# The attention's query chain in two requests, and the keys' scaling half a piece later

## The chip, the cores and the metric

The kernel runs on one core of a Trainium2 chip. The metric is the device time of one execution in microseconds; for comparison stands the median of several timed executions without a profile. One further execution was taken with the hardware profiler, and all views of the profile come from it. The engines are named as the profile names them: PE is TensorE (matmuls and transposes, PEld its weight loads), ACT is ScalarE, DVE is VectorE, POOL is GpSimd, SP only issues transfers.

## The reference

A decoder trunk of two layers over 256 tokens of width 2048: a retention layer and its MLP, then keys and values from a compressed latent, and an attention layer with its MLP. What the change touches is the attention, with 16 heads, 128 unrotated and 64 rotated columns per head:

```python
    k_nope = rms_norm(kv[..., :MLA_NOPE_DIM], k_nope_norm)
    ...
    c_q = rms_norm(h @ w_dq, q_norm)
    q = (c_q @ w_uq).reshape(b, s, H, MLA_NOPE_DIM + MLA_ROPE_DIM)
    q_nope = rms_norm(q[..., :MLA_NOPE_DIM], q_nope_norm)
    q_pe = apply_rope(rms_norm(q[..., MLA_NOPE_DIM:], q_pe_norm), cos[:, :, None], sin[:, :, None])
    ...
        sc = jnp.einsum('bhqd,bkhd->bhqk', qn, k_nope) + jnp.einsum('bhqr,bkr->bhqk', qp, k_pe)
        sc = sc.astype(jnp.float32) * scale
        sc = jnp.where(kpos[None, :] <= qpos[:, None], sc, -jnp.inf)
        p = jax.nn.softmax(sc, axis=-1).astype(v.dtype)
        return jnp.einsum('bhqk,bkhd->bqhd', p, v)
    ...
    return o @ w_o
```

## The kernel before

**Weights and pieces.** All products run in float32 accuracy from two parts of each operand: a high part (a cast to fp32r on ACT, L188) and a low part, which is what the cast left over (a subtraction on DVE, L189). PE multiplies high by high, high by low and low by high (L248 to L250 in `piece`). A weight matrix comes in pieces. Each piece is one transfer on SP's queue into one of three `raw` buffers and is used in two halves; each half gets a `wh` and a `wl` tile, of which there are five each. A half of the query's up-projection `uq` is 768 columns wide and feeds 12 matmuls; a half of the output projection `wo` has 1024 columns, and 12 matmuls as well. So PE needs the cast and the subtraction of a half before it starts that half.

**What sets the order.** The helper work between the matmuls is asked for by a small clock. `stream` advances it by half a piece after each half (`tick(0.5)`), `later(n, fn)` puts a function n pieces ahead, and it is run, that is, its instructions are recorded, when the clock gets there. From the recorded program the framework makes one queue for each engine and puts neighbours that don't depend on each other in an order of its own; every engine then works through its queue strictly in order. An instruction at the head of a queue that waits holds up everything behind it. Names in the profile are those of the tiles; in the order's rows the first digit behind a name is the head pair b and the second the token tile t.

**Keys.** `keyed` runs once for each of the eight head pairs (two heads each, two token tiles of 128). ACT scales keys and values out of PSUM, DVE squares and sums the keys (L964, L965) and forms mean plus epsilon (`kn_m`, L177), POOL raises it to the power -1/2 (`kn_r`, L178), and DVE scales the keys with it (L970). Two pieces later they are transposed (`kntp`) and split.

**Queries.** `query` runs behind the three pieces of `uq` for each head pair. ACT takes the queries and their squares out of PSUM (L994, L996), DVE sums the squares (L997, L998) and forms mean plus epsilon (`qn_m`), POOL makes the power (`qn_r`), and DVE scales the queries (L1005), rotates the 64 rotated columns (`pe_rope`, L863 to L866) and splits them (`qpp`, L1014, L1015). 3.5 pieces later (2.5 for the last pair) `turn` transposes both parts on PE (`qntp`, `qptp`) and makes `qt` (L1021, then cast and split) and `qpe` (L1026).

**Scores and softmax.** `score` follows 2.5 pieces behind (1.5 and 1 for the last two pairs). PE makes the scores `s` (L1041 to L1046), DVE adds the mask (L1051) and takes the maxima (`mx`, L1056), ACT the exponentials with their sums (L1061), DVE the reciprocals (`inv`, L1062), ACT scales (L1067). Then PE transposes the probabilities (`ptp`, L1074), ACT copies them (`pt`, L1076), `values` multiplies by the values (`ao`, L1085, L1086), and ACT copies the result (`ou`, L1089), which is split for `wo`. `ptp` and `ao` take turns in two PSUM banks, so each must wait until ACT has emptied the bank of the last but one.

Of the kernel before, what the change touches and what calls it, by code (L numbers as in the profile page):

```python
# [16 lines left out]
ALU = mybir.AluOpType  # L17
# [18 lines left out]
P = 128  # L36
NT = 2
# [6 lines left out]
NOPE, ROPE, MV, KVR, QR = 128, 64, 128, 512, 1536  # L44
# [22 lines left out]
def yoco(ctx: ExitStack, tc: tile.TileContext, a):  # L67
    nc = tc.nc
# [3 lines left out]
    def f2k(shape, name, dtype=F32):  # L72
        return pool.tile([P, *shape], dtype, tag="f2k", bufs=14, name=name)

    def small(w, name):
        return pool.tile([P, w], F32, tag="small", bufs=36, name=name)
# [12 lines left out]
    def act_tile(name, dtype=F32R):  # L89

        return pool.tile([P, 2, 2, S], dtype, tag="act", bufs=24, name=name)
# [5 lines left out]
    def later(n, fn):  # L97
        queue.append((clock[0] + n, next(count), fn))
# [60 lines left out]
    def gain(col):  # L159
        return gains[:, col : col + 1]  # L160
# [10 lines left out]
    def rstds(total, sizes, name):  # L171

        w = total.free_size()
        m, r = small(w, f"{name}_m"), small(w, f"{name}_r")
        view = m.rearrange("p (t i h) -> p t i h", t=NT, i=len(sizes))
        for i, n in enumerate(sizes):
            nc.vector.tensor_scalar(view[:, :, i], total[:, :, i], 1.0 / n, EPS, op0=ALU.mult, op1=ALU.add)  # L177
        nc.gpsimd.tensor_tensor(r, m, neg_half[:, :w], op=ALU.pow)  # L178
        return r.rearrange("p (t i h) -> p t i h", t=NT, i=len(sizes))
# [5 lines left out]
    def split(h, l, src, scale=None):  # L185

        if scale is None:
            nc.scalar.copy(h, src)  # L188
            return nc.vector.tensor_tensor(l, src, h.bitcast(F32), op=ALU.subtract)  # L189
        nc.scalar.activation(h, src, AF.Copy, scale=scale)  # L190
        return nc.vector.scalar_tensor_tensor(
            l, src, scale, h.bitcast(F32), op0=ALU.mult, op1=ALU.subtract
        )
# [8 lines left out]
    def transposed(srcs, name):  # L202

        tp = bank("tp", [2, S], name)
        for j in range(2):
            for t in range(NT):
                nc.tensor.transpose(tp[:, j, t * P : (t + 1) * P], srcs(t, j), ident)
        return tp
# [509 lines left out]
    act, r = [], []  # L718
# [3 lines left out]
    def ret_projected(h, qk, gate, v, s):  # L722

        wait = 0 if h else 8

        def keyed(acc):
            ret_rope(acc, qk, f"rk{h}", max(wait - 4, 0))
            later(2 if h else 5.5, ret_scores(h, qk, s))

        gemm_t(a["ret_w_qk"], h * 2, act0, KD, f"rq{h}", lambda acc: ret_rope(acc, qk, f"rq{h}", max(wait - 2, 0)))  # L730
        gemm_t(a["ret_w_qk"], (RH + h) * 2, act0, KD, f"rk{h}", keyed)
# [125 lines left out]
    def pe_rope(dst, u, src, t, i, heads):  # L857


        def tab(j, lo, n):  # L860
            return pe_tabs[t][i][:, j, lo : lo + n].unsqueeze(1).to_broadcast([P, heads, n])

        nc.vector.tensor_tensor(dst, src, tab(0, 0, 64), op=ALU.mult)  # L863
        nc.vector.tensor_tensor(u[:, :, 0:32], src[:, :, 32:64], tab(1, 0, 32), op=ALU.mult)
        nc.vector.tensor_tensor(u[:, :, 32:64], src[:, :, 0:32], tab(1, 32, 32), op=ALU.mult)
        nc.vector.tensor_tensor(dst, dst, u, op=ALU.add)  # L866
# [85 lines left out]
    def keyed(acc, b):  # L952
        if b % 2 == 0:
            vs.append(act_tile(f"v{b}", F32))
        vt = vs[-1][:, b % 2].rearrange("p t (h c) -> p t h c", h=2)
        v_s.append(vt)
        kr = []
        s2 = small(2 * NT, f"skn{b}").rearrange("p (t i h) -> p t i h", t=NT, i=1)
        for t in range(NT):
            src = acc[t].rearrange("p (h c) -> p h c", h=2)  # L960
            k = f2k([2, 2, NOPE], f"kn{b}{t}")
            nc.scalar.activation(k[:, 0], src[:, :, 0:NOPE], AF.Copy, scale=rc[t])
            nc.scalar.activation(vt[:, t], src[:, :, NOPE:], AF.Copy, scale=rc[t])
            nc.vector.tensor_tensor(k[:, 1], k[:, 0], k[:, 0], op=ALU.mult)  # L964
            nc.vector.reduce_sum(s2[:, t, 0], k[:, 1], axis=AX.X)  # L965
            kr.append(k)
        rn = rstds(s2, [NOPE], f"kn{b}")
        for t in range(NT):
            k = kr[t]
            nc.vector.tensor_tensor(  # L970
                k[:, 1], k[:, 0], rn[:, t, 0].unsqueeze(2).to_broadcast([P, 2, NOPE]), op=ALU.mult
            )

        def turn():
            tp = transposed(lambda t, j: kr[t][:, 1, j], f"kntp{b}")
            kt = act_tile(f"kt{b}")
            split(kt[:, 0], kt[:, 1], tp, gain(G_KN))
            k_t.append(kt)

        later(2, turn)  # L980

    for b in range(8):
        gemm(a["mla_w_kv_up"], b, ckv, 4, 512, f"ku{b}", lambda acc, b=b: keyed(acc, b))
# [3 lines left out]
    o_act = []  # L987

    def query(acc, b):
        qr, qu = [], []  # L990
        sq = small(4 * NT, f"sq{b}").rearrange("p (t i h) -> p t i h", t=NT, i=2)
        for t in range(NT):
            q = f2k([2, 192], f"qs{b}{t}")
            nc.scalar.activation(q.rearrange("p h c -> p (h c)"), acc[t], AF.Copy, scale=rq[t])  # L994
            u = f2k([2, 192], f"qu{b}{t}")
            nc.scalar.activation(u.rearrange("p h c -> p (h c)"), acc[t], AF.Square, scale=rq[t])  # L996
            nc.vector.reduce_sum(sq[:, t, 0], u[:, :, 0:NOPE], axis=AX.X)  # L997
            nc.vector.reduce_sum(sq[:, t, 1], u[:, :, NOPE:], axis=AX.X)  # L998
            qu.append((q, u))
        r = rstds(sq, [NOPE, ROPE], f"qn{b}")  # L1000
        for t in range(NT):
            q, u = qu[t]
            for i, cols in enumerate((slice(0, NOPE), slice(NOPE, NOPE + ROPE))):
                n = cols.stop - cols.start
                nc.vector.tensor_tensor(  # L1005
                    q[:, :, cols], q[:, :, cols], r[:, t, i].unsqueeze(2).to_broadcast([P, 2, n]), op=ALU.mult
                )
            flat = u.rearrange("p h c -> p (h c)")
            pe = flat[:, 0 : 2 * ROPE]
            tmp = flat[:, 2 * ROPE : 4 * ROPE].rearrange("p (h c) -> p h c", h=2)  # L1010
            pe_rope(pe.rearrange("p (h c) -> p h c", h=2), tmp, q[:, :, NOPE:], t, 1, 2)
            parts = f2k([2, 2, ROPE], f"qpp{b}{t}", F32R)
            pe = pe.rearrange("p (h c) -> p h c", h=2)
            nc.vector.tensor_copy(parts[:, :, 0], pe)  # L1014
            nc.vector.tensor_tensor(parts[:, :, 1], pe, parts[:, :, 0].bitcast(F32), op=ALU.subtract)  # L1015
            qr.append((q, parts.bitcast(F32)))

        def turn():
            tp = transposed(lambda t, j: qr[t][0][:, j, 0:NOPE], f"qntp{b}")
            raw = f2k([2, S], f"qt{b}")  # L1020
            nc.scalar.activation(raw, tp, AF.Copy, scale=gqn)  # L1021
            qt = [f2k([2, S], f"qt{b}{i}", F32R) for i in range(2)]
            split(qt[0], qt[1], raw)
            tp = transposed(lambda t, j: qr[t][1][:, j].rearrange("p i c -> p (i c)"), f"qptp{b}")
            qpe = f2k([2, S], f"qpe{b}", F32R)
            nc.scalar.copy(qpe, tp)  # L1026
            later(2.5 if b < 6 else (1.5 if b < 7 else 1), lambda: score(b, qt, qpe))

        later(2.5 if b == 7 else 3.5, turn)

    def score(b, qt, qpe):

# [60 lines left out]
    for b in range(8):  # L1093
        gemm(a["mla_w_uq"], b * 3, cq, 12, Q_NB, f"uq{b}", lambda acc, b=b: query(acc, b))

    ss = square_sums(NB, "ss3")
    act, r = [], []
# [107 lines left out]
```

## Time and profile before

| | us |
|---|---|
| timed executions (three) | 2480.28, 2480.34, 2482.13; median 2480.34 |
| profiled execution, device time | 2490.9 |
| its span, first to last instruction | 2489.1 |
| keys' up-projection on PE begins | 1505.6 |
| `uq` begins | 1552.6 |
| first `wo` product, behind the scores of pair 5 | 1685.3 |
| `wo` in pairs (`wop`) begins | 1752.3 |
| DVE idle until POOL's `qn_r`, eight times | 13.5 |
| mean granted clock of PE over the span | 0.996 |

The profiled execution is 10.6 us longer than the median of the timed ones; what is read off the profile is compared with its own time. A row of the timeline gives start and length in us, engine, source line, operation, the tile written and those read, and, in brackets, how long the engine sat idle before it and which instruction ended that. A row of stretches gives the bounds, the length, then for each engine its busy time and its number of instructions, the granted clock of PE (1.00 is full), the share of the DMA engines and GB/s.

### The profile page before, as it was taken

The numbers are of one execution on the slowest core, as the hardware profiler recorded it, in microseconds if no ns is written. First come the engines' busy times: TensorE is split into PE (matmuls) and PEld (weight loads), VectorE is DVE, ScalarE is ACT, GpSimd is POOL, SyncE is SP. The second block draws the span as 40 slices with busy tenths as digits, with TensorE's granted clock in tenths as the row PEclk, the third lists the DMA queues.
The fourth block names the chain that finished last, engine by engine and source line by source line (L and its number), as shares of the span: only waits on it lengthen the run. The fifth ranks groups of instructions, "written<-read, shape, count | busy, mean of one in ns | idle before, by whom it ended". The sixth has DMA issues, their size and how long they took to land.

```text
span 2489.1 us, 31657 instructions
## 1 busy us (share of the span) xinstructions
PE 2458.4 (99%) x11614; PEld 2064.2 (83%) x11614; DVE 2199.3 (88%) x2894; ACT 1647.9 (66%) x2301; POOL 232.0 (9%) x287
## 2 busy tenths in 40 slices
PE   9999999999999999999999999999999999999999
PEld 7888887888888888888888888997888788888887
DVE  7899989989899989989999998776999899899896
ACT  6566656556676767666667777666677567676663
POOL 6200001000000010010110001100000100100100
PEclk9999999999999999999999999999999999999999
DMA  8555568555565685785785565444555866866864
GB/s 311 201 196 190 200 190 252 190 194 207 197 236 187 201 251 207 226 238 197 245 261 204 190 207 177 156 148 156 192 204 200 237 214 199 252 201 225 256 212 167
DMA packets 93403, 521.04 MB, mean 209 GB/s; under 512 B 11072, under 2 KB 12224, under 8 KB 40000
## 3 DMA queue, kind: packets, MB, share of 16 engines
q1 hardware_dynamic: 71856, 472.83, 54.2%
q0 software_dynamic: 21248, 46.15, 8.8%
q8 instruction: 91, 1.49, 0.2%
q14 instruction: 64, 0.52, 0.1%
q10 hardware_dynamic: 144, 0.05, 0.0%
HBM read 479.14 MB, written 39.85 MB: 209 GB/s over the span
## 4 chain that ended last, share of the span: by engine, by line
PE 81%; DVE 7%; DMA 5%; issue 3%; POOL 2%; ACT 2%; DVEq 0%; SPq 0%; ACTq 0%; POOLq 0%
PE u_c L365 7%; PE u_c L366 6%; PE u_c L364 6%; PE d_c L365 5%; PE d_c L366 5%; PE d_c L364 5%; PE rp_c L365 3%; PE rp_c L366 3%; PE rp_c L364 3%; PE rk_acc L276 2%; PE rq_acc L276 2%; PE u_p L366 2%; PE u_p L365 2%; DMA d_raw<-in_mlp_w 2%; PE u_p L364 2%
## 5 line engine op out<-in xcount | busy, mean ns | idle before, releaser
L189 DVE TENSOR_TENSOR d_wl<-d_raw,d_wh 128x1024 fp32r<-128x1024 f32 (+1 forms) x256 | 279.1, 1115 | 27.8 <-ACT d_wh L188 27.8
L188 ACT CAST d_wh<-d_raw 128x1024 fp32r<-128x1024 f32 (+1 forms) x256 | 241.8, 975 | 83.6 <-PE d_c L366 49.5
L189 DVE TENSOR_TENSOR u_wl<-u_raw,u_wh 128x1024 fp32r<-128x1024 f32 (+1 forms) x256 | 277.3, 1111 | 16.8 <-ACT u_wh L188 16.8
L188 ACT CAST u_wh<-u_raw 128x1024 fp32r<-128x1024 f32 (+1 forms) x256 | 240.6, 972 | 70.3 <-PE u_c L366 51.0
L365 PE MATMUL u_c<-u_wl,n 128*128 128x512 f32 x712 | 278.6, 391 | 4.0 <-DVE u_wl L189 4.0
L364 PE MATMUL u_c<-u_wh,n 128*128 128x512 f32 x712 | 278.9, 392 | 0.0
L366 PE MATMUL u_c<-u_wh,n 128*128 128x512 f32 x712 | 278.0, 391 | 0.0
L365 PE MATMUL d_c<-d_wl,hid 128*128 128x512 f32 x660 | 257.8, 391 | 4.1 <-DVE d_wl L189 4.0
L364 PE MATMUL d_c<-d_wh,hid 128*128 128x512 f32 x660 | 259.1, 393 | 0.0
L366 PE MATMUL d_c<-d_wh,hid 128*128 128x512 f32 x660 | 257.7, 390 | 0.0
L188 ACT CAST u_wh<-u_u 128x1024 fp32r<-128x1024 f32 x104 | 107.7, 1054 | 112.0 <-DVE u_u L328 53.3
L188 ACT CAST d_wh<-d_u 128x1024 fp32r<-128x1024 f32 x100 | 104.0, 1055 | 100.4 <-DVE d_u L328 55.8
L365 PEld LDWEIGHTS u_c<-u_wl,n 128*128 128x128 f32 x712 | 134.1, 188 | 33.9 <-DVE u_wl L189 6.7
L366 PEld LDWEIGHTS u_c<-u_wh,n 128*128 128x128 f32 x712 | 134.0, 188 | 27.6
L364 PEld LDWEIGHTS u_c<-u_wh,n 128*128 128x128 f32 x712 | 134.2, 188 | 27.4
L365 PEld LDWEIGHTS d_c<-d_wl,hid 128*128 128x128 f32 x660 | 124.4, 189 | 31.2 <-DVE d_wl L189 6.0
L188 ACT CAST rp_wh<-rp_raw 128x1024 fp32r<-128x1024 f32 x112 | 103.9, 945 | 66.3 <-PE rp_c L366 43.1
L366 PEld LDWEIGHTS d_c<-d_wh,hid 128*128 128x128 f32 x660 | 124.2, 188 | 25.7
L364 PEld LDWEIGHTS d_c<-d_wh,hid 128*128 128x128 f32 x660 | 124.4, 188 | 25.4
L189 DVE TENSOR_TENSOR u_wl<-u_u,u_wh 128x1024 fp32r<-128x1024 f32 x104 | 124.0, 1220 | 9.5 <-ACT u_wh L188 9.4
L189 DVE TENSOR_TENSOR rp_wl<-rp_raw,rp_wh 128x1024 fp32r<-128x1024 f32 x112 | 118.4, 1085 | 4.1 <-ACT rp_wh L188 3.9
L189 DVE TENSOR_TENSOR d_wl<-d_u,d_wh 128x1024 fp32r<-128x1024 f32 x100 | 118.9, 1219 | 2.5 <-ACT d_wh L188 2.4
(566 smaller groups left out, 6579.0 us busy)
## 6 DMA issues: line engine op xcount, KB each, us to landing
u_raw<-in_mlp_w SPq DMA_DIRECT2D x128, 1024.0 KB, 5.5
d_raw<-in_mlp_w SPq DMA_DIRECT2D x120, 1024.0 KB, 4.9
rp_raw<-in_ret_w_gv SPq DMA_DIRECT2D x56, 1024.0 KB, 4.9
ro_raw<-in_ret_w_out SPq DMA_DIRECT2D x32, 1024.0 KB, 5.0
uq_raw<-in_mla_w_uq SPq DMA_DIRECT2D x24, 768.0 KB, 4.2
rq_raw<-in_ret_w_qk SPq DMA_DIRECT2D x16, 1024.0 KB, 5.4
rk_raw<-in_ret_w_qk SPq DMA_DIRECT2D x16, 1024.0 KB, 4.9
xh<-d_c POOLq DMA_DIRECT2D x48, 256.0 KB, 6.2
```

The costliest lines, as they stand in the source:

```text
L188: nc.scalar.copy(h, src)
L189: return nc.vector.tensor_tensor(l, src, h.bitcast(F32), op=ALU.subtract)
L276: nc.tensor.matmul(acc[f], wh[:, cols], a.rearrange("p i s -> p (i s)"), start=k == 0, stop=k == nk - 1)
L364: nc.tensor.matmul(dst, ah, bh, start=n == 0, stop=False)
L365: nc.tensor.matmul(dst, ah, bl, start=False, stop=False)
L366: nc.tensor.matmul(dst, al, bh, start=False, stop=n == total[key] - 1)
```

## The change

`query` ends with the request for the power. Scaling, rotation and split become a function `rotated`, asked for 1.5 pieces later (1 for the last pair). `turn` is asked for by `rotated`, 2 pieces behind it (1.5 for the last pair), so it keeps its place at 3.5 (2.5) pieces. In `keyed` the scaling of the keys is asked for half a piece later; its `turn` stays at 2 pieces. No instruction is added or taken away on any engine, and the queues of SP and POOL keep their order.

```diff
--- before.py
+++ after.py
@@ -965,11 +965,15 @@
             nc.vector.reduce_sum(s2[:, t, 0], k[:, 1], axis=AX.X)
             kr.append(k)
         rn = rstds(s2, [NOPE], f"kn{b}")
-        for t in range(NT):
-            k = kr[t]
-            nc.vector.tensor_tensor(
-                k[:, 1], k[:, 0], rn[:, t, 0].unsqueeze(2).to_broadcast([P, 2, NOPE]), op=ALU.mult
-            )
+
+        def normed():
+            for t in range(NT):
+                k = kr[t]
+                nc.vector.tensor_tensor(
+                    k[:, 1], k[:, 0], rn[:, t, 0].unsqueeze(2).to_broadcast([P, 2, NOPE]), op=ALU.mult
+                )
+
+        later(0.5, normed)
 
         def turn():
             tp = transposed(lambda t, j: kr[t][:, 1, j], f"kntp{b}")
@@ -987,7 +991,7 @@
     o_act = []
 
     def query(acc, b):
-        qr, qu = [], []
+        qu = []
         sq = small(4 * NT, f"sq{b}").rearrange("p (t i h) -> p t i h", t=NT, i=2)
         for t in range(NT):
             q = f2k([2, 192], f"qs{b}{t}")
@@ -998,6 +1002,10 @@
             nc.vector.reduce_sum(sq[:, t, 1], u[:, :, NOPE:], axis=AX.X)
             qu.append((q, u))
         r = rstds(sq, [NOPE, ROPE], f"qn{b}")
+        later(1 if b == 7 else 1.5, lambda: rotated(b, qu, r))
+
+    def rotated(b, qu, r):
+        qr = []
         for t in range(NT):
             q, u = qu[t]
             for i, cols in enumerate((slice(0, NOPE), slice(NOPE, NOPE + ROPE))):
@@ -1026,7 +1034,7 @@
             nc.scalar.copy(qpe, tp)
             later(2.5 if b < 6 else (1.5 if b < 7 else 1), lambda: score(b, qt, qpe))
 
-        later(2.5 if b == 7 else 3.5, turn)
+        later(1.5 if b == 7 else 2, turn)
 
     def score(b, qt, qpe):
 
```

What that does to the queues is seen at three places; in the rows of the change the lines below the edit stand 8 higher.

DVE at the end of the query stage, around pair 7's mean (`qn7_m`) and pair 5's mask (`p50`, `p51`). Before, these rows stand behind the whole of pair 7's rotation, whose first row (`qs70`) needs the power of `qn7_m`:

```order
L866 TENSOR_TENSOR qu71_15629<-qu71_15629 128x128
L189 TENSOR_TENSOR wo01_wl1_15890<-wo01_raw_15853,wo01_wh1_15889 128x1024
L1014 COPY qpp71_15653<-qu71_15629 128x2x64
L1051 TENSOR_TENSOR p50_15677<-s5_15656,cst_62 128x256
L1015 TENSOR_TENSOR qpp71_15653<-qu71_15629,qpp71_15653 128x2x64
L1051 TENSOR_TENSOR p51_15678<-s5_15656,cst_62 128x512
L1056 TENSOR_REDUCE mx5_15681<-p50_15677 128x2
L1056 TENSOR_REDUCE mx5_15681<-p51_15678 128x2
L189 TENSOR_TENSOR qt61_15729<-qt6_15726,qt60_15728 128x512
```

Now:

```order
L177 TENSOR_SCALAR qn7_m_15633<-sq7_15620 128x2x2
L1059 TENSOR_TENSOR p50_15659<-s5_15638,cst_62 128x256
L177 TENSOR_SCALAR qn7_m_15633<-sq7_15620 128x2x2
L1059 TENSOR_TENSOR p51_15660<-s5_15638,cst_62 128x512
L1064 TENSOR_REDUCE mx5_15663<-p50_15659 128x2
L1064 TENSOR_REDUCE mx5_15663<-p51_15660 128x2
L1013 TENSOR_TENSOR qs70_15621<-qs70_15621,qn7_r_15634 128x2x128
L1013 TENSOR_TENSOR qs70_15621<-qs70_15621,qn7_r_15634 128x2x64
L1013 TENSOR_TENSOR qs71_15627<-qs71_15627,qn7_r_15634 128x2x128
```

Mask and maxima of pair 5 have moved ahead of pair 7's scaled queries, right behind the mean; `qt61` and the low part `wo01_wl1` follow behind the rotation.

DVE in pair 2's rotation, at the low part of the second half of pair 3's last piece of `uq` (`uq32_wl1`: the digits are the pair and its piece, the 1 the second half). Before:

```order
L1051 TENSOR_TENSOR p01_14586<-s0_14564,cst_62 128x512
L1056 TENSOR_REDUCE mx0_14589<-p00_14585 128x2
L1056 TENSOR_REDUCE mx0_14589<-p01_14586 128x2
L189 TENSOR_TENSOR qt11_14631<-qt1_14628,qt10_14630 128x512
L189 TENSOR_TENSOR uq32_wl1_14710<-uq32_raw_14691,uq32_wh1_14709 128x768
L1062 RECIPROCAL inv0_14591<-den0_14590 128x4
L189 TENSOR_TENSOR uq40_wl0_14817<-uq40_raw_14814,uq40_wh0_14816 128x768
```

Now:

```order
L1070 RECIPROCAL inv0_14573<-den0_14572 128x4
L189 TENSOR_TENSOR qt11_14613<-qt1_14610,qt10_14612 128x512
L1022 COPY qpp20_14663<-qu20_14531 128x2x64
L1022 COPY qpp21_14672<-qu21_14537 128x2x64
L1023 TENSOR_TENSOR qpp20_14663<-qu20_14531,qpp20_14663 128x2x64
L1023 TENSOR_TENSOR qpp21_14672<-qu21_14537,qpp21_14672 128x2x64
L189 TENSOR_TENSOR uq32_wl1_14710<-uq32_raw_14691,uq32_wh1_14709 128x768
L189 TENSOR_TENSOR uq40_wl0_14799<-uq40_raw_14796,uq40_wh0_14798 128x768
```

The low part stood ahead of the softmax's reciprocal; now it stands behind the reciprocal, behind the split `qt11` and behind the four rows of `qpp`.

ACT at the same place, with the semaphores that a row waits for. Before:

```order
L188 COPY uq32_wh0_14693<-uq32_raw_14691 128x768 [waits DMAHW7_49,DVE_49]
L188 COPY uq32_wh1_14709<-uq32_raw_14691 128x768 [waits DVE_49,PE_49]
L1021 ACTIVATE qt1_14628<-qntp1_14623,gqn_86 128x512 [waits DVE_49,PE_49]
L188 COPY qt10_14630<-qt1_14628 128x512 [waits Activation_49]
L1061 ACT_TABLE_LOAD
L1061 ACTIVATE p00_14585,den0_14590<-p00_14585,mx0_14589 128x128 [waits DVE_49]
L1061 ACTIVATE p00_14585,den0_14590<-p00_14585,mx0_14589 128x128
```

Now:

```order
L188 COPY uq32_wh0_14693<-uq32_raw_14691 128x768 [waits DMAHW7_49,DVE_49]
L1069 ACT_TABLE_LOAD [waits DVE_49]
L1069 ACTIVATE p00_14567,den0_14572<-p00_14567,mx0_14571 128x128 [waits Activation_49]
L1069 ACTIVATE p00_14567,den0_14572<-p00_14567,mx0_14571 128x128
L1069 ACTIVATE p01_14568,den0_14572<-p01_14568,mx0_14571 128x256 [waits DVE_49]
L1069 ACTIVATE p01_14568,den0_14572<-p01_14568,mx0_14571 128x256
L1029 ACTIVATE qt1_14610<-qntp1_14605,gqn_86 128x512 [waits PE_49]
L1075 ACTIVATE p00_14567<-p00_14567,inv0_14573 128x128 [waits DVE_49]
L1075 ACTIVATE p00_14567<-p00_14567,inv0_14573 128x128 [waits Activation_49]
L1075 ACTIVATE p01_14568<-p01_14568,inv0_14573 128x256 [waits Activation_49] x2
L188 COPY qt10_14612<-qt1_14610 128x512 [waits Activation_49]
L188 COPY uq32_wh1_14709<-uq32_raw_14691 128x768
```

The table for the exponentials and the exponentials themselves moved ahead of the cast `uq32_wh1` and of `qt1`, and the table load now carries a wait for DVE. Near the end of the stage ACT's row for `wo02_wh0`, which stood behind the copies `pt50` and `pt51`, stands ahead of them.

## The prediction

> **What bounds the kernel now.** I began with the page's busy times:
>
> ```profile
> span 2489.1 us, 31657 instructions
> PE 2458.4 (99%) x11614; PEld 2064.2 (83%) x11614; DVE 2199.3 (88%) x2894; ACT 1647.9 (66%) x2301; POOL 232.0 (9%) x287
> ```
>
> PE (TensorE) sets the time: only where PE waits, or runs at a lower clock, can another order of the same work win or lose. So the second view is what PE waited for from 1500 to 1760 us, the stretch that the change touches (total, times, longest):
>
> ```profile
> PE ptp L1074 <- ACT p L1067: 3.6, 2, 3.4
> PE ptp L1074 <- ACT ou L1089: 2.2, 3, 0.9
> PE ao L1085 <- ACT pt L1076: 1.0, 1, 1.0
> PE ptp L1074 <- ACT qpe L1026: 0.3, 2, 0.2
> ```
>
> All of it is at the transposes of the softmax (ptp) and the product behind them (ao); nothing stands there for the keys. The third view, busy time by stretch (after the bounds: length, PE, PEld, DVE, ACT, POOL, then the granted clock), prices it:
>
> ```profile
> 1642.80:1696.90 54.10, 51.44 (x312) 47.51 (x311) 39.83 (x104) 36.72 (x75) 9.22 (x11) 1.00 0.50 170
> 1695.96:1699.38 3.42, 1.24 (x6) 0.70 (x4) 3.02 (x8) 1.50 (x7) 0.00 (x0) 1.00 0.96 380
> 1696.90:1709.62 12.72, 8.14 (x32) 7.00 (x31) 6.53 (x9) 8.50 (x20) 0.00 (x0) 0.60 0.56 208
> 1700.56:1709.62 9.06, 7.84 (x30) 7.00 (x31) 4.28 (x4) 5.82 (x10) 0.00 (x0) 0.50 0.39 128
> 1945.14:1948.55 3.41, 1.44 (x7) 0.88 (x6) 3.38 (x4) 0.88 (x2) 0.00 (x0) 1.00 0.05 14
> 1948.55:1951.96 3.41, 3.41 (x9) 2.65 (x9) 3.41 (x5) 1.06 (x2) 0.85 (x1) 0.50 0.65 171
> ```
>
> Idle PE: 54.10 - 51.44 = 2.66 us, then 12.72 - 8.14 = 4.58 us. After the second gap the granted clock is 0.50, for 9.06 us of which 7.84 are work.
>
> The fourth view is the timeline of that gap, on PE, DVE, ACT and POOL:
>
> ```profile
> 1696.59 0.39 PE L249 MATMUL wo_acc<-wo_wl,ot 128*128 128x512 f32 x1
> 1696.82 0.39 PE L250 MATMUL wo_acc<-wo_wh,ot 128*128 128x512 f32 x1
> 1700.56 0.48 PE L1074 MATMUL ptp<-cst,p 128*128 128x128 f32 x1 [3.36 <-ACT p L1067]
> 1701.25 1.33 PE L1074 MATMUL ptp<-cst,p 128*128 128x128 f32 x5 [0.21 <-ACT p L1067]
> 1703.91 1.22 PE L1085 MATMUL ao<-pt,v 128*128 128x256 f32 x2 [1.01 <-ACT pt L1076]
> ...
> 1690.01 0.29 DVE L177 TENSOR_SCALAR qn_m<-sq 128x4 f32<-128x4 f32 x2
> 1692.08 0.96 DVE L1005 TENSOR_TENSOR qs<-qs,qn_r 128x256 f32<-128x256 f32 x3 [1.78 <-POOL qn_r L178]
> 1696.24 0.42 DVE L1051 TENSOR_TENSOR p<-s,cst 128x256 f32<-128x256 f32 x1
> 1697.38 1.00 DVE L1056 TENSOR_REDUCE mx<-p 128x2 f32<-128x256 f32 x2
> 1699.77 0.18 DVE L1062 RECIPROCAL inv<-den 128x4 f32<-128x4 f32 x1 [0.80 <-ACT p L1061]
> ...
> 1697.88 0.40 ACT L1061 ACTIVATE p<-p,mx 128x128 f32<-128x128 f32 x1 [6.25 <-DVE mx L1056]
> 1699.64 0.56 ACT L1026 CAST qpe<-qptp 128x512 fp32r<-128x512 f32 x1
> 1700.11 1.49 ACT L1067 ACTIVATE p<-p,inv 128x128 f32<-128x128 f32 x4
> ...
> 1690.38 1.66 POOL L178 TENSOR_TENSOR qn_r<-qn_m,neg_half 128x8 f32<-128x8 f32 x1 [18.02 <-DVE qn_m L177]
> ```
>
> DVE stood 1.78 us behind POOL's power for the last head pair (pair 7), then did that pair's rotation, and only then the mask (p<-s) of pair 5, though PE had computed pair 5's scores before the wo products that end here. ACT sat 6.25 us for the maxima, PE 3.36 us for ACT.
>
> **The change part by part.**
>
> *The last gap.* The new order has p50 right behind the mean of pair 7, at 1690.1 instead of 1696.24. From p50 to the first exponential took 1697.88 - 1696.24 = 1.64 us, so that starts at 1691.8, on an idle ACT; four take 1699.64 - 1697.88 = 1.76, to 1693.5. The power ends at 1692.04, hidden behind masks and maxima (1696.24 to 1698.38). Scaling the probabilities (1.49) ends by 1695.5, with 0.5 allowed for qt6 that now stands before it, while PE's last wo product (0.23 apart) is issued until 1697.05. The row of 3.6 us goes.
>
> *The wait that comes instead.* ao4 takes the PSUM bank of ptp50, so pt50's copy must be done. ACT's order now has the cast of wo02 ahead of that copy, and the cast needs the buffer that PE gives back at the end of the same wo product:
>
> ```profile
> 1704.12 1.05 ACT L188 CAST wo_wh<-wo_raw 128x1024 fp32r<-128x1024 f32 x1
> 1703.38 0.84 ACT L1076 COPY pt<-ptp 128x384 f32<-128x384 f32 x2
> ```
>
> A cast of 1.05 and one copy of about 0.5, against what PE has to do from ptp50 to ao4: 1703.91 - 1700.56 - 0.21 - 1.01 = 2.13 us at half clock, 1.07 at full. PE waits about 0.5, where it waited 1.01; I take 0.5 (0 to 1.0).
>
> *The half clock* goes with the gap: 7.84 us of work at 0.50 take 3.92 at full clock, so 3.92. The stretches to 1699.38 and 1948.55 had PE busy 1.24 and 1.44 of 3.4 us, and the clock was 0.50 behind both; through the short waits of 1642.80 to 1696.90 it was 1.00. Waits of 0.5 to 1 leave 2.4 busy or more, so none follows.
>
> *The three short waits.* The 2.66 us are the rows of ou and qpe (2.2 and 0.3) and rounding. ptp's second bank waited for ou, which ACT copied behind the softmax. Exponentials and scaling now start 1696.24 - 1690.1 = 6 us earlier in each pair, so this idle goes too (0 to 2.66). Idle time also hides a part of each wait: from 1697.05 to 1700.56 are 3.51 us and 3.36 are shown. For eight waits at 0.15, 1.2 us (0 to 1.6).
>
> *What is late next: the low part of a piece's second half.* uq32_wl1, uq62_wl1 and so on now stand on DVE behind softmax, rotation, the reciprocal and qt's split, which wait for ACT. The rows (busy and mean ns by group; then for pair 5 of the queries its mean and PE's first use of the low part):
>
> ```profile
> L1021 ACT ACTIVATE qt<-qntp,gqn 128x512 f32<-128x512 f32 x7 | 4.9, 699 | 0.0
> L188 ACT CAST qt<-qt 128x512 fp32r<-128x512 f32 x7 | 4.3, 612 | 0.1
> L189 DVE TENSOR_TENSOR qt<-qt,qt 128x512 fp32r<-128x512 f32 x7 | 4.8, 688 | 1.3 <-ACT qt L188 1.3
> L1015 DVE TENSOR_TENSOR qpp<-qu,qpp 128x128 fp32r<-128x128 f32 x16 | 4.5, 284 | 0.0
> ...
> 1650.31 0.29 DVE L177 TENSOR_SCALAR qn_m<-sq 128x4 f32<-128x4 f32 x2
> 1659.95 0.33 PE L249 MATMUL uq_acc<-uq_wl,cq 128*128 128x384 f32 x1
> ```
>
> From 1650.4: exponentials from 1652.1 to 1653.9, then qt 0.70, scaling 1.49, cast 0.61, split 0.69, four qpp at most 1.1, the low part 0.95: 5.5 us laid end to end, 1659.4; neighbours on an engine overlap by about 0.1 each (the four scalings start 0.3 to 0.4 apart), so nearer 1658.7. Before 1659.95 either way: no wait in pairs 3 to 7. In pair 2 the chain is longer, by ACT's table load, which now waits for the first maximum, and by a slower power:
>
> ```profile
> 1594.55 2.31 POOL L178 TENSOR_TENSOR qn_r<-qn_m,neg_half 128x8 f32<-128x8 f32 x1 [11.05 <-DVE qn_m L177]
> 1596.90 0.96 DVE L1005 TENSOR_TENSOR qs<-qs,qn_r 128x256 f32<-128x256 f32 x3 [1.53 <-POOL qn_r L178]
> 1598.62 1.28 ACT L1061 ACT_TABLE_LOAD   x1
> 1602.70 0.95 DVE L189 TENSOR_TENSOR uq_wl<-uq_raw,uq_wh 128x768 fp32r<-128x768 f32 x1
> 1605.73 0.33 PE L249 MATMUL uq_acc<-uq_wl,cq 128*128 128x384 f32 x1
> ```
>
> p00 at 1597.4 (two of the three qs), its maximum 1598.8, table 1600.1, exponentials 1601.9, and the same 5.5, less the overlaps 4.7: 1606.6 to 1607.4, where PE wants it at 1605.73. A wait of 0.8 to 1.6; I take 0.8, as in pair 5.
>
> The power is 2.31 there, with a split of uq beside it, and 1.66 beside an idle DVE. The Trainium skill ("SBUF — State Buffer", section "Who interferes with whom") says that a DVE instruction with two SBUF inputs shuts out GpSimd's reads; by that rule the masks, which read PSUM and one SBUF operand, leave the power at 1.66. Stretched by 0.65 all the same, the power would end at 1692.7 and the low parts come 0.65 later at most, about level with PE's use.
>
> *The keys.* Sixteen products move half a piece behind kn_r. DVE waited 4.9 us there in all, PE never:
>
> ```profile
>   DVE kn L970: 4.9, 8
> ```
>
> PE's work covers it, and the transposes of the keys keep 1.5 pieces behind it: 0; without that cover it would be up to 4.9. The orders of SP and POOL, their DMAs among them, stay as they were.
>
> *Sum against the profiled execution (2490.9 us, 2489.1 of them the span):* 2.66 + 4.58 + 3.92 + 1.2 = 12.4 gained, 0.5 + 0.8 = 1.3 paid, net 11.1: 2479.8. The timed runs have a median of 2480.34, 10.6 below the profiled one; I take the same gain there: **2469.2 us**.
>
> **The rivals.**
>
> *The timed runs had no half clock (0.12).* The clock rows are of one execution, and no timed run shows its clock. Against it, 1.24 busy of 3.42 is lower than in the other stretch that lost its clock, and the gap is in every run. Then the gain is 11.1 - 3.9 = 7.2: 2473.1. The Trainium skill ("TensorE: Matmul & The Clock Gate", section "HAM oscillation — how this bites in real kernels") has the clock fall after idle gaps over about 3.4 us; by that the gap of 3.36 is a borderline case. The trace differs: 1.97 us idle of 3.41 were enough at 1948.55.
>
> *Late low parts: slower (0.06).* If ACT comes to the exponentials 4 us later than I put it, in pairs 2 to 7, the low parts are done 2.7 us after PE's use in each: 2480.3 - 11.1 + 6 x 2.7 = 2485.4. It decides from the point where the low part ends behind PE's use (1659.95 for pair 5). For it: qt and the casts on ACT wait for PE's transposes and buffers. Against it: ACT idled 6.25 us exactly there.
>
> *The gap moves (0.12).* ao4, or a low part, waits some 3 us and the clock halves again: 3 + 3.9 come back, and with a second such wait up to 10; 2475 to 2480. For it: ao4's bank hangs on two releases in a row. Against it: the cast and the copy need 1.55 us, no more. That the program does not do what the edit says is excluded by its order, where p50 stands ahead of the scaled queries.
>
> **How the numbers follow.** The forecast has 0.70. Its own terms reach from 12.4 + 0.4 = 12.8 (nothing paid, all hidden parts) to 11.2 - 1.0 - 1.6 = 8.6 (none hidden, both new waits at their bounds): 2467.5 to 2471.8. The range adds the first rival, the nearer part of the third, and 1.5 us below for the spread of the timed runs: **2466.0 to 2476.0**. Within 0.2% (5.0 us; less can't be told from no change in this kernel) begins at 2475.4: two thirds of the third rival, 0.08. Slower 0.06. Faster: 0.70 + 0.12 + 0.04 = 0.86.
>
> **What would show it.** In the changed profile: DVE's qs without waits for POOL from pair 3 on; ACT's first exponential of pair 5 without a wait near 6 us; PE with no idle at ptp, about 0.5 at ao4 and 0.8 at the low part of uq3; a clock of 1.00 from 1680 to 1720. Wrong if PE waits at the low parts of several pairs, if ao4 waits over 1.5 us, or if the clock still halves in this stage.

## The result, and the profile after

| | before | changed |
|---|---|---|
| median of 13 executions each (one of the changed kernel's is the profiled one), us | 2480.34 (2475.36 to 2487.55) | 2473.35 (2461.8 to 2478.78) |
| ratio, 95% interval | | 0.9963 (0.9948 to 0.9978) |
| profiled execution, device time / span, us | 2490.9 / 2489.1 | 2474.0 / 2472.2 |
| first `uq` product to first `wop` product, us | 199.6 | 188.7 |
| mean granted clock over the span | 0.996 | 1.000 |

The change is faster by 0.37%, 9.2 us with an interval of 5.5 to 12.9 (2480.34 times one minus each bound of the ratio; the ratio is that of the means, and the two medians lie only 7.0 us apart). The forecast was 2469.2 us, within 2466.0 to 2476.0; the median measured, 2473.35, lies in that range. The forecast gain was 11.1 us. Over the whole program the spread of single executions is about as large as the gain, so the sharper measure below is the **stretch** from the first `uq` product to the first `wop` product, read off PE's timeline in each profile. Its ends in the changed kernel:

```profile
1554.71 0.42 PE L248 MATMUL uq_acc<-uq_wh,cq 128*128 128x384 f32 x1
...
1743.45 0.48 PE L364 MATMUL wop_c<-wop_wh,ot 128*128 128x512 f32 x1
```

They are 188.7 us apart, 10.9 less than before. The two profiled spans differ by 16.9; the other 6 us lie outside the stretch, in parts that the change leaves alone. Behind it the profile of before has PE waits of 7.0 us and two clock halvings, the changed one waits of 2.7 us and none. These are not the change's.

PE's waits between 1500 and 1760 us (total, times, longest) are now these, in place of four rows with 7.1 us:

```profile
PE uq_acc L249 <- DVE uq_wl L189: 0.9, 1, 0.9
PE ao L1093 <- ACT pt L1084: 0.5, 1, 0.5
```

All waits at ptp are gone. The two that are left are those that the prediction named, 0.8 and 0.5 there. The busy times in the corresponding stretches (length, PE, PEld, DVE, ACT, POOL, clock, DMA share, GB/s), moved by the 2.1 us by which `uq` begins later:

```profile
1644.90:1699.00 54.10, 53.64 (x334) 51.06 (x333) 43.39 (x109) 41.48 (x88) 9.22 (x11) 1.00 0.60 206
1699.00:1720.00 21.00, 21.00 (x122) 18.30 (x121) 11.25 (x20) 14.45 (x37) 0.00 (x0) 1.00 0.42 152
```

PE idles 54.10 - 53.64 = 0.46 us where it idled 2.66, and after that not at all, and the clock stays at 1.00. The place of the last gap, on the timeline of the changed kernel:

```profile
1683.58 0.59 ACT L998 ACTIVATE qs<-uq_acc,cq_r 128x384 f32<-128x384 f32 x1
1684.58 0.40 PE L248 MATMUL wo_acc<-wo_wh,ot 128*128 128x512 f32 x1
1686.22 0.41 DVE L1059 TENSOR_TENSOR p<-s,cst 128x256 f32<-128x256 f32 x1
1687.74 0.40 ACT L1069 ACTIVATE p<-p,mx 128x128 f32<-128x128 f32 x1 [2.15 <-DVE mx L1064]
1688.49 0.96 DVE L1013 TENSOR_TENSOR qs<-qs,qn_r 128x256 f32<-128x256 f32 x3 [0.27 <-POOL qn_r L178]
1696.37 0.82 PE L1082 MATMUL ptp<-cst,p 128*128 128x128 f32 x6
```

The mask of pair 5 starts before the scaled queries of pair 7, ACT waits 2.15 us for the maxima instead of 6.25, and the transposes (ptp) follow without a wait. But note the first two rows. ACT takes pair 7's queries out of PSUM at 1683.58, 1.0 us before the first `wo` product. Before the change it did so 2.2 us after that product:

```profile
1685.25 0.40 PE L248 MATMUL wo_acc<-wo_wh,ot 128*128 128x512 f32 x1
1687.46 0.57 ACT L994 ACTIVATE qs<-uq_acc,cq_r 128x384 f32<-128x384 f32 x1
```

So the whole chain of the last pair began 3.2 us earlier on PE's own scale. The prediction had left it where it was. Whether the last gap was the last pair's own, as predicted, or was handed on from the pairs before it is what most of the experiments are about.

### The profile page after: what moved, and what is told of

Read it like the earlier page. It is cut to its first block, busy times and chain, and to the rows that moved or that the text cites. A ratio compares the mean times of both kernels' runs of the same rounds, so it can differ in the third digit from the quotient of the medians.

```text
span 2472.2 us, 31666 instructions
## 1 busy us (share of the span) xinstructions
PE 2450.6 (99%) x11614; PEld 2059.0 (83%) x11614; DVE 2196.2 (89%) x2894; ACT 1648.7 (67%) x2301; POOL 233.6 (9%) x287
## 3 DMA queue, kind: packets, MB, share of 16 engines
q8 instruction: 91, 1.49, 0.2%
## 4 chain that ended last, share of the span: by engine, by line
PE 86%; DVE 6%; DMA 4%; POOL 2%; issue 1%; ACT 1%; SPq 0%; DVEq 0%; ACTq 0%
PE u_c L365 6%; PE u_c L366 6%; PE u_c L364 6%; PE d_c L365 6%; PE d_c L366 6%; PE d_c L364 6%; PE rp_c L364 3%; PE rp_c L366 3%; PE rp_c L365 3%; PE rk_acc L276 2%; PE rq_acc L276 2%; DMA u_raw<-in_mlp_w 2%; PE d_p L364 2%; PE d_p L365 2%; PE d_p L366 2%; PE u_p L364 2%
```

## The experiments

Each kernel was profiled once. "Stretch" is always from the first `uq` to the first `wop` product. The price of the half clock is half of the PE work that ran at 0.50 inside the stretch, and "at full clock" is the stretch without it. Ratios are to the kernel before, run on the same chip. The kernels split for some pairs only have the keys' scaling where the change has it.

| run | ratio (95%) | stretch | half clock costs | at full clock |
|---|---|---|---|---|
| before | | 199.6 | 3.9 | 195.7 |
| before again | 0.9998 (0.9985 to 1.0012) | 199.3 | 3.8 | 195.5 |
| keys only | 1.0002 (0.9991 to 1.0012) | 198.3 | 2.7 | 195.6 |
| the change | 0.9963 (0.9948 to 0.9978) | 188.7 | 0 | 188.7 |
| query only | 0.9961 (0.9948 to 0.9975) | 188.8 | 0 | 188.8 |
| pair 7 only | 0.9979 (0.9970 to 0.9988) | 195.2 | 1.7 | 193.5 |
| pairs 0 to 6 | 0.9970 (0.9956 to 0.9985) | 190.8 | 0 | 190.8 |
| no power | 0.9955 (0.9938 to 0.9972) | 189.4 | 0 | 189.4 |
| later still | 0.9963 (0.9948 to 0.9978) | 188.7 | 0 | 188.7 |
| many gaps | 1.0375 (1.0352 to 1.0398) | 188.7 | 0 | 188.7 |
| pair 6 only | 1.0003 (0.9987 to 1.0019) | 195.1 | 1.5 | 193.6 |
| pairs 0 to 5 | 0.9989 (0.9977 to 1.0001) | 195.5 | 2.8 | 192.7 |
| from pair 3 on | 0.9958 (0.9941 to 0.9975) | 187.5 | 0 | 187.5 |
| both new waits off | 0.9955 (0.9940 to 0.9969) | 186.8 | 0 | 186.8 |

**Before, again.** No edit.

> The kernel before, unchanged, profiled a second time. It asks how much of what the first profile showed comes back. If the gaps belong to the order of the queues: the stretch from the first uq product to the first wop product is again 199.7 us (within 0.5), PE waits 3.4 us at ptp for pair 5's probabilities, and ratio 1.000. If the half clock behind the gap is an accident of where the gap falls: the clock stays 1.00 there this time, and the stretch is about 195.8 (199.7 less the 3.9 us of half clock).

The gaps came back to a tenth of a microsecond: the four rows of PE's waits between 1500 and 1760 us are those that the prediction shows, figure for figure. So did the half clock behind them. In the stretches of this second profile PE is busy 1.38 us of 3.4, then the clock is 0.50 for 10.2 us with 7.65 us of work:

```profile
1702.10:1705.50 3.40, 1.38 (x7) 0.80 (x5) 3.15 (x8) 1.34 (x7) 0.00 (x0) 1.00 0.91 307
1705.50:1715.70 10.20, 7.65 (x30) 6.81 (x31) 4.46 (x5) 7.15 (x15) 0.00 (x0) 0.50 0.51 186
```

So the stretch is a steady measure (199.6 and 199.3), while the whole span is not (2489.1 and 2484.7).

**The keys alone, and the queries alone.** The first leaves `query` as it was; the second puts the keys' scaling back (the edit shown is the second's):

```diff
-        later(0.5, normed)
+        normed()
```

> Only the keys' scaling is moved; the query chain stands as before. Theory: PE never waited for the keys, so 0: stretch uq to wop 199.7, ratio 1.000, DVE's 4.9 us behind kn_r shorter but worth nothing. Rival: part of the gain comes from here, up to 4.9 us, ratio down to 0.998.

> Only the query chain is split; the keys' scaling stands at its old place. Theory: the whole gain, stretch 188.7 us as in the change, the same two waits (0.9 at the low part of uq3, 0.5 at ao4), ratio as the change has it, 0.996. Rival (the keys matter): stretch 0.5 us or more longer than 188.7.

The keys' part is worth nothing: the stretch at full clock is that of before, the ratio 1.0002. Even DVE's wait, expected to shrink, stayed (total, times, longest):

```profile
DVE kn L972 <- POOL kn_r L178: 4.9, 8, 1.1
```

The stretch itself came out 1.3 us shorter than before's, though PE's waits were the same. Its profile shows why: this time the clock was at 0.50 for 6.8 us and not 10.2.

```profile
1703.10:1709.90 6.80, 5.46 (x20) 4.62 (x20) 3.58 (x3) 5.10 (x10) 0.00 (x0) 0.50 0.34 106
1709.95:1713.00 3.05, 3.05 (x22) 2.84 (x22) 1.83 (x4) 0.79 (x2) 0.00 (x0) 1.00 0.56 236
```

The queries' part alone gives the whole gain, with the same two waits of 0.9 and 0.5.

**The last pair alone, and all but the last.** In the first the split is made for pair 7 only, in the second for 0 to 6 only:

```diff
-        later(1 if b == 7 else 1.5, lambda: rotated(b, qu, r))
+        if b == 7:      # second kernel: b < 7
+            later(1 if b == 7 else 1.5, lambda: rotated(b, qu, r))
+        else:
+            rotated(b, qu, r)
```

with `turn` kept at its old distance from `query` in both, and the keys' scaling half a piece later as in the change.

> The query chain is split for pair 7 alone; pairs 0 to 6 and the keys... the keys' scaling stays half a piece later. My prediction's account: the last gap comes from pair 7's own rotation standing ahead of pair 5's mask, so the 3.4 us at ptp and the half clock go (8.5 us), the three short waits of 2.7 us stay: stretch about 199.7 - 8 = 191.7. Rival (the lateness is handed on from pair to pair: ACT takes pair 7's queries out of PSUM late because pair 4's softmax came late): mask and maxima come earlier but ACT is late all the same, PE still waits 2 us or more at ptp or ao4, stretch 193 or more; if the clock still halves, 196.

> The reverse: the query chain is split for pairs 0 to 6, and pair 7 stands as before, its rotation ahead of pair 5's mask. My prediction's account: the short waits go (2.7 us and hidden parts) and the last gap stays with its half clock: stretch about 199.7 - 3.5 + 0.9 = 197, and PE still waits 3.4 us at ptp50. Rival (the lateness is handed on): with pair 4's softmax on time ACT takes pair 7's queries out earlier, the gap at ptp50 shrinks to 1 us or less, some 1.6 us remain at ao4, no half clock: stretch 190 to 191.

Pair 7 alone: the wait at ptp50 is gone, but 2.3 us stand at ao4, and the short waits are all there (total, times, longest):

```profile
PE ao L1097 <- ACT pt L1088: 2.3, 1, 2.3
PE ptp L1086 <- ACT ou L1101: 2.2, 3, 0.9
PE ptp L1086 <- ACT qpe L1038: 0.7, 3, 0.3
```

On its timeline the mask stands early, as the order has it, yet ACT takes the queries 2.2 us after the first `wo` product, as before:

```profile
1684.90 0.40 PE L248 MATMUL wo_acc<-wo_wh,ot 128*128 128x512 f32 x1
1687.10 0.58 ACT L998 ACTIVATE qs<-uq_acc,cq_r 128x384 f32<-128x384 f32 x1
1688.72 0.41 DVE L1063 TENSOR_TENSOR p<-s,cst 128x256 f32<-128x256 f32 x1
...
1697.36 2.94 ACT L188 CAST wo_wh<-wo_raw 128x1024 fp32r<-128x1024 f32 x3
1700.20 0.85 ACT L1088 COPY pt<-ptp 128x384 f32<-128x384 f32 x2
1700.73 0.70 PE L1097 MATMUL ao<-pt,v 128*128 128x256 f32 x2 [2.27 <-ACT pt L1088]
```

ACT, still late, had three casts of `wo` to make up, 2.94 us of them ahead of the copy of pt50, and ao4 waited for that. In the changed kernel the same row of casts had caught up with PE: the last of them waits 0.98 us for a `wo` product. The clock was 0.50 for one stretch of 3.4 us behind the wait at ao4. The forecast of 191.7 was missed by 3.5 us, though the softmax itself came as the prediction had it: the first exponential 6.0 us after the first `wo` product, where the prediction's 1691.8 is 6.5.

All but the last: pair 7's rotation still stands ahead of the mask, and the gap is gone all the same:

```profile
PE ao L1097 <- ACT pt L1088: 1.4, 1, 1.4
PE uq_acc L249 <- DVE uq_wl L189: 0.9, 1, 0.9
PE ptp L1086 <- ACT p L1079: 0.5, 2, 0.4
```

On the timeline ACT takes pair 7's queries 1.0 us before the first `wo` product, and DVE waits its full 1.78 us for the power as it did before, but 3.2 us earlier against PE:

```profile
1682.21 0.60 ACT L998 ACTIVATE qs<-uq_acc,cq_r 128x384 f32<-128x384 f32 x1
1683.22 0.40 PE L248 MATMUL wo_acc<-wo_wh,ot 128*128 128x512 f32 x1
1686.85 0.96 DVE L1017 TENSOR_TENSOR qs<-qs,qn_r 128x256 f32<-128x256 f32 x3 [1.78 <-POOL qn_r L178]
1690.08 0.42 DVE L1063 TENSOR_TENSOR p<-s,cst 128x256 f32<-128x256 f32 x1
```

The stretch has 4.9 us of the 7.0 that the change gains at full clock, and all of the half clock, without touching the last pair. Part of the 4.9 are the short waits, which this run was expected to remove. What counts for the last gap is PE's wait at ptp50, 0.4 us in place of 3.4, at the price of 1.4 at ao4 in place of 1.0. The lateness was handed on, and ACT's rows show how. The first exponential of pair 4, before and with pairs 0 to 6 split:

```profile
1676.84 0.40 ACT L1061 ACTIVATE p<-p,mx 128x128 f32<-128x128 f32 x1 [4.44 <-DVE mx L1056]
1668.47 0.40 ACT L1073 ACTIVATE p<-p,mx 128x128 f32<-128x128 f32 x1 [2.20 <-DVE mx L1068]
```

It comes 8.4 us ahead of the first `wo` product before and 14.8 us ahead of it here. Before, ACT then works through its queue up to its copy of pair 7's queries with 0.31 us of idle time in 10.6; here it has caught up, and waits 0.37 us for PE and 0.57 us for DVE on the way.

**The power left out.** The kernel before, in its old order, with the queries scaled by mean plus epsilon instead of its power -1/2:

```diff
-        r = rstds(sq, [NOPE, ROPE], f"qn{b}")
+        r = small(4 * NT, f"qn{b}_m").rearrange("p (t i h) -> p t i h", t=NT, i=2)
+        for i, n in enumerate((NOPE, ROPE)):
+            nc.vector.tensor_scalar(r[:, :, i], sq[:, :, i], 1.0 / n, EPS, op0=ALU.mult, op1=ALU.add)
```

> The kernel before, in its old order of requests, but the queries' power on POOL is left out: the queries are scaled by mean plus epsilon itself, so their normalization is not the reference's. DVE then never waits for POOL in the query chain. If the gain comes from the wait for the power (the 1.5 to 1.8 us that DVE stood in each pair): most of the gain of the change is had without moving anything, stretch 189 to 191. If it comes from the order (rotation, 4.2 us of work ahead of the mask, whoever is waited for): the last gap only shrinks by 1.8 us, stretch 195 or more.

Two waits are left, 1.4 at ao4 and 0.4 at ptp; the stretch is 189.4:

```profile
PE ao L1087 <- ACT pt L1078: 1.4, 1, 1.4
PE ptp L1076 <- ACT p L1069: 0.4, 1, 0.4
```

In its order the rotation of pair 7 still stands ahead of pair 5's mask. So 1.7 us less on DVE in each pair (13.5 in eight) gives nearly all of the gain with nothing moved on purpose: what the rotation did ahead of the mask mattered less than that it waited there. The run does not separate the two fully: the framework's order shifts a little when an operation goes, and 0.7 of the 7.0 us that the change gains at full clock are missing.

**Later still.** The split's second part one piece later again:

```diff
-        later(1 if b == 7 else 1.5, lambda: rotated(b, qu, r))
+        later(2 if b == 7 else 2.5, lambda: rotated(b, qu, r))
...
-        later(1.5 if b == 7 else 2, turn)
+        later(0.5 if b == 7 else 1, turn)
```

> The change with the query chain's second part asked for one piece later again (2.5 pieces, 2 for pair 7; the transposes keep their place). If the delay itself matters: the transposes, now 1 piece (0.5 for pair 7) behind the request, or the low parts behind the rotation, make PE wait; 1 us or more longer than 188.7 in the stretch. If any delay that puts masks and maxima ahead of the scaled queries is as good: 188.7 within 0.3, and the same two waits.

188.7 us, and the same two waits of 0.9 and 0.5. Between these two delays the amount does not matter; what matters is that masks and maxima come ahead of the instruction that waits.

**Many gaps.** The change, with ACT's cast of the first part of twelve pieces of `ro` done ten times:

```diff
             wl = pool.tile([P, 1024], F32R, tag="wl", bufs=5, name=f"{name}_wl{part}")
+            if name[:2] == "ro" and int(name[4:]) in (1, 4, 7) and part == 0:
+                for _ in range(9):
+                    nc.scalar.copy(wh[:, : n * 512], src)
```

> The change, with ACT's cast of the first part of twelve pieces of ro (the retention's output projection) done ten times instead of once, so that PE must wait there for ACT many times, in all some 90 us, with waits of 1 to 6 us close together. It asks whether timed executions lose the clock as the profiled one does. The profile will show how much work ran at clock 0.50 behind those waits. If timed runs have it too: their median lies within 10 us of the profiled time. If not: it lies below the profiled time by half of the work that the trace has at clock 0.50, some 30 us or more if the clock halves behind each group of waits.

PE waited there 48.0 us for ACT (total, times, longest). Its whole idle time between 300 and 860 us is 67.6 (560.0 less 492.4 busy), less than the 90 that I expected:

```profile
PE ro_p L367 <- ACT ro_wh L188: 26.4, 11, 3.7
PE ro_c L367 <- ACT ro_wh L188: 21.6, 11, 5.8
```

The clock was 0.50 in eleven stretches between 339 and 828 us, 88.7 us long in all, with 56.9 us of PE work in them. The two longest:

```profile
766.20:779.90 13.70, 7.43 (x20) 5.56 (x21) 7.92 (x11) 11.60 (x21) 0.00 (x0) 0.50 0.23 74
431.65:441.89 10.24, 6.62 (x15) 4.44 (x15) 6.28 (x6) 6.72 (x9) 0.86 (x1) 0.50 0.39 107
```

The profiled execution took 2582.6 us and the three others 2574.5, 2576.5 and 2577.9. Without the half clock they would lie 28 us lower than the profiled one (half of 56.9); they lie 5 to 8 us lower. So executions other than the profiled one lose the clock as well. The mean granted clock that the results list for each execution says the same: 0.981 to 0.982 in all four here; 0.996 to 0.999, on average 0.998, in 27 executions of the kernel before; 0.998 to 1.000, on average 0.9995, in 13 of the change.

**Pair 6 alone, and pairs 0 to 5.** The same edit as for pair 7, with another condition:

```diff
-        if b == 7:
+        if b == 6:      # second kernel: b < 6
```

> The query chain is split for pair 6 alone (the keys' scaling as in the change). Split for pairs 0 to 6 it had removed the gap at ptp50. If the lateness is handed on in one step (pair 6's rotation holds up pair 4's softmax, and that holds up ACT's copy of pair 7's queries): pair 6 alone does the same, PE waits 0.5 us at ptp50 and 1.4 at ao4, no half clock, only the short waits of pairs 2 and 3 stay: stretch 190.8 + 2 = 192 to 193. If it adds up over several pairs: PE still waits 1.5 us or more at ptp50.

> The reverse of the run with pair 6 alone within pairs 0 to 6: split for 0 to 5, pairs 6 and 7 as before. If the lateness is handed on in one step from pair 6: the gap of 3.4 us at ptp50 is all there with its half clock, the short waits are gone but for pair 4's: stretch 196 or more. If it adds up over several pairs: the gap is shorter than 3.4 us but 2 us or more, and whether the clock halves then is open: 192 without, 194 to 196 with it.

Pair 6 alone leaves 2.1 us at ptp50 and 1.4 at ao4, pairs 0 to 5 leave 2.9 and 1.0 (first the one, then the other):

```profile
PE ptp L1086 <- ACT p L1079: 2.4, 2, 2.1
PE ao L1097 <- ACT pt L1088: 1.4, 1, 1.4
PE ptp L1086 <- ACT ou L1101: 1.3, 2, 0.7
```

```profile
PE ptp L1086 <- ACT p L1079: 3.3, 2, 2.9
PE ao L1097 <- ACT pt L1088: 1.0, 1, 1.0
PE uq_acc L249 <- DVE uq_wl L189: 0.9, 1, 0.9
```

So it is not one step. Read off the timelines as above, ACT's copy of pair 7's queries starts, against the first `wo` product, at +2.2 before, +1.8 with 0 to 5 split, +0.9 with 6 alone, and -1.0 with 0 to 6. PE's own waits between its last `uq` product and its first `wo` product blur this scale. Another zero is the end of the last `uq` product of the same pair. For pair 7 before, that product is this one, and ACT's copy at 1687.46 starts 6.5 us behind its end:

```profile
1680.63 0.34 PE L250 MATMUL uq_acc<-uq_wh,cq 128*128 128x384 f32 x1
```

By this scale the copies start late by these us (in pairs 0 to 2 they are on time in every run):

| run | pair 3 | pair 4 | pair 5 | pair 6 | pair 7 |
|---|---|---|---|---|---|
| before | 2.1 | 3.3 | 4.6 | 4.7 | 6.5 |
| the change | 3.7 | 2.8 | 1.7 | 1.5 | 1.8 |
| pair 6 only | 1.9 | 3.1 | 4.4 | 4.7 | 3.7 |
| pairs 0 to 5 | 3.6 | 2.6 | 1.5 | 1.5 | 4.6 |
| no power | 1.5 | 1.5 | 1.5 | 1.5 | 3.6 |

Before, the lateness grows from pair to pair. The change starts later at pair 3 and works it off. With pairs 0 to 5 split it has gone back to 1.5 by pair 6, and pair 6's rotation alone then makes pair 7 2.8 us later than in the change. With pair 6 alone split, 1.9 us are still handed on from the pairs ahead. The two make the 4.7 us of before: it adds up over pairs, with the largest single step at pair 6.

The timed runs do not confirm pair 6's gain (ratio 1.0003, where the 4.5 us of the stretch would make 0.998). Of the 4.5, 2.4 belong to a shorter half clock in this one profile (1.5 us of price for 3.9), and the mean clock of its ten executions is 0.998, as before.

**From pair 3 on, and both new waits off.** The split for pairs 3 to 7 only; then, in a second kernel and in addition, the product with the values of pair 4 later:

```diff
-        if b == 7:
+        if b > 2:
...
-            later(2 if b < 5 else 0.5 if b > 5 else 1, lambda: values(b, pt))
+            later(3 if b == 4 else 2 if b < 5 else 0.5 if b > 5 else 1, lambda: values(b, pt))
```

> The change, but pairs 0 to 2 keep the old request (scaling, rotation and split at once); pairs 3 to 7 are split. The low part of uq3's last half then stands ahead of the softmax of pair 0 with its table load again. Theory: PE's wait of 0.9 us there goes and nothing else moves: stretch 187.9, only the 0.5 at ao4 is left. Rival: without the split pair 0's softmax is late again, and a wait at ptp comes in its place: stretch 188.7 or more.

> As the run that splits from pair 3 on, and the product with the values of pair 4 (ao4) is asked for one piece later, 3 instead of 2, so that it no longer waits for the copies of ptp50 that stand behind the cast of wo02 on ACT. Theory: both waits that the change brought are gone, no PE wait over 0.2 us from uq to wop: stretch 187.4, ratio to the kernel before 0.9955. Rival: ao4's later place makes ou4 and so ot4 late for wo, a new wait there: stretch 188 or more.

The first leaves one wait, 0.5 at ao4. The second leaves none: PE is busy for the whole stretch.

```profile
1553.60:1740.40 186.80, 186.80 (x1122) 177.46 (x1121) 138.91 (x327) 131.52 (x264) 21.48 (x20) 1.00 0.48 167
```

Against the change that is 1.9 us in the stretch. It leaves nothing of the computation out and is the shortest of all there; its ratio to before, 0.9955, overlaps that of the change, 0.9963, so the timed runs alone cannot tell the two apart.

## Why the prediction was right, and where its reasons were not

The sum against the trace, term by term. Shown waits gone: 7.1 us (3.6 + 2.2 + 1.0 + 0.3). New waits: 0.9 + 0.5 = 1.4. Half clock gone: 3.9. That makes 9.6, and the stretch gained 10.9. The remaining 1.3 have the size of the hidden parts of the waits, for which the forecast had 1.2; no row shows them one by one.

- *The wait that comes instead* (0.5 at ao4) and *the low part of uq3* (0.8) were measured as 0.5 and 0.9. No other low part waits, as worked out for pair 5. Both mechanisms were confirmed by taking them away: the split from pair 3 on removed the 0.9, the later ao4 the 0.5.
- *The half clock* went, all 3.9 us. The rival that timed runs never had it falls with the run of many gaps. The mean clocks agree with that: 0.9995 less 0.998 over 2480 us is 3.7 us of clock lost by the kernel before and not by the change, or some 7.4 us at 0.50 (an estimate from rounded means, for the whole program). That it fell behind this very gap was seen in three profiles only. Its length, though, is not fixed: with PE's waits in the stretch the same, it was 10.2, 10.2 and 6.8 us in three profiles.
- *The three short waits* went entirely.
- *The keys* are worth 0, as said; the products' half piece did not even change DVE's wait.
- *The power beside the masks* stayed short: 1.64 to 1.66 us in pairs 3 to 7, though POOL now runs beside masks and maxima. The Trainium skill ("SBUF — State Buffer", section "Who interferes with whom") says that a DVE instruction with two SBUF inputs shuts out GpSimd's reads; the masks have one operand in PSUM and the maxima one input, so the trace agrees. In pairs 0 to 2, beside the split of `uq` with two inputs in SBUF, it takes 2.25 to 2.32 us. Pair 7's power:

```profile
1686.80 1.66 POOL L178 TENSOR_TENSOR qn_r<-qn_m,neg_half 128x8 f32<-128x8 f32 x1 [15.50 <-DVE qn_m L177]
```

- *The last gap* is the step that failed, with the right size: its reason was only half of the cause. It said that pair 7's mask came late because pair 7's rotation stood ahead of it, with the mean of pair 7 fixed at 1690.1. That the rotation stands in the way was right: with pair 7 alone split the first exponential comes 6.0 us after the first `wo` product, where the forecast had 6.5. But this gains only 2.2 us at full clock and moves the wait to ao4 (2.3 us, where the forecast had 0.5). Splitting all the others, with pair 7's rotation where it was, takes the wait at ptp50 down to 0.4 us. What the step overlooked is that the mean itself hung on a queue of late work: each pair's softmax, held up behind a rotation, kept ACT busy later, so ACT took the next queries out later, and so on down to pair 7, 3.2 us in all against the first `wo` product. Either split alone removes nearly all of the 3.4 us at ptp50: the first exponential comes 12.6 us after the first `wo` product before, 8.5 with the others split, 6.0 with pair 7 split, and 3.2 with both. That the price came out right is in part luck: the 0.5 at ao4 was worked out with one cast ahead of the copy of pt50. With pair 7 alone split ACT is still late and has three to do there; the 0.5 holds only because the change splits the other pairs as well, which the step did not count on.
- *DVE's qs "without waits for POOL from pair 3 on"* holds to within 0.3 us in two pairs; pairs 0 to 2 keep 1.5 each, 5.2 in all for 13.5 before.

The timed gain of 9.2 has 11.1 within its interval. The forecast was made against a profile with the half clock at its longest; an execution with 6.8 us of it, as in the keys-only run, has 1.2 us less to gain.

## What to carry to other kernels

A wait on a side engine that costs the bound engine (here PE) little or nothing in most rounds can still add up: an in-order queue hands the delay to the next round, and it shows where the slack ends. Before a gap is priced by the instructions next to it, look one and two rounds back and ask whether the first instruction of its chain starts on time against the bound engine's own work. Put the work that somebody else waits for ahead of an instruction that must wait; in the two delays tried here, how far ahead did not matter.

## What the runs showed of the hardware

In these profiles the clock of PE halves after a stretch of 3.41 us with too little PE work; no idle time of 3.4 us in one piece is needed. Inside an execution all changes of the clock lie whole multiples of 3.41 us apart, so the execution can be cut into stretches at these steps. In the fourteen profiles 29 such stretches were followed by 0.50 (the ends of the executions left out), all with PE busy 1.62 us or less (under 48%). Of some 10,000 that were not followed by it, one had less than 1.71 (1.49, where records may be missing); the first 11 us, for which not every profile records the clock, are left out. The two nearest to the border, one from the run with pairs 0 to 5 and one from the run with many gaps, each with the stretch that follows:

```profile
1213.30:1216.70 3.40, 1.61 (x8) 1.02 (x7) 3.37 (x4) 1.22 (x2) 0.00 (x0) 1.00 0.08 20
1216.70:1220.10 3.40, 3.40 (x10) 2.63 (x9) 3.40 (x5) 1.04 (x1) 0.86 (x1) 0.50 0.54 130
```

```profile
2254.40:2257.80 3.40, 1.70 (x8) 1.12 (x7) 3.37 (x4) 1.53 (x2) 0.00 (x0) 1.00 0.27 59
2257.80:2261.20 3.40, 3.40 (x16) 2.79 (x15) 3.40 (x5) 1.87 (x2) 0.86 (x1) 1.00 0.45 87
```

The Trainium skill ("TensorE: Matmul & The Clock Gate", section "HAM oscillation — how this bites in real kernels") has the clock fall after idle gaps over about 3.4 us. The runs differ: behind the gap of 3.4 us it fell in both profiles of the kernel before, but also behind the 2.3 us of the run with pair 7 alone, where PE was busy 1.4 us of the stretch. Apart from the end of an execution, each period at 0.50 was one to four such stretches long (3.4 to 13.7 us); the longest had waits in them (7.43 us busy of 13.70), those of one stretch hardly any (3.1 us busy or more).
